# Key tiles turned behind softmax shares, roots written in place, a fifth weight tile and a store on another queue, in a decoder layer on one core

## The chip, the cores and the metric

The kernel runs on 1 core of one Trainium2 chip. The metric is the device time of one execution in microseconds (us). The core has five engines that run side by side, each through its own instruction stream, in order: TensorE (PE, with its weight loads PEld), VectorE (DVE), ScalarE (ACT), GpSimd (POOL) and SyncE (SP), which here only issues transfers. They wait for each other through semaphores.

## The reference

One layer of a hybrid decoder is computed for a prompt of 512 rows and for 8 samples of 4 rows each (32 rows), with the same weights, model width 1024. Cut to what matters:

```python
h = rms_norm(x, g_mix_pre); z = h @ w_in          # mLSTM heads and differential attention read z
mix = concat([mlstm(z), diff_attention(z)])
x = x + rms_norm(mix @ w_out, g_mix_post)
h = rms_norm(x, g_mem_pre)                        # cross-attention, 4 heads x 256, 256 memory tokens
s = einsum('bqhd,bkhd->bhqk', (h @ w_mq), mk) * 256 ** -0.5
x = x + rms_norm((softmax(s) applied to mv) @ w_mo, g_mem_post)
u = rms_norm(x, g_ffn_pre) @ w_up                 # width 2 x 2752, causal depthwise conv of width 3
f = (silu(g) * a) @ w_down
y = x + rms_norm(f, g_ffn_post)
```

where `rms_norm(x, g)` is `x * rsqrt(mean(x * x) + 1e-6) * g`. For the prompt, `mk` and `mv` come from a memory of 256 rows (`rms_norm(mem) @ w_mk`, `@ w_mv`). For each of the 8 samples they are cached: `cache_mem_k` and `cache_mem_v`, 256 tokens x 1024 numbers for each sample. Caches and states are returned too.

## The kernel before, in words

**Order of the work.** The program is written with a tile framework that is told to plan the order by a simulated timeline (L2059, `schedule_with_timeline_sim=True`). What is written earlier has priority, but each engine's final instruction order is the planner's, and it may take an instruction ahead of others if it thinks that its inputs are ready first. Buffers are taken from pools in the same plan. `tc.issue_after(ins)` around a block puts the block's instructions on the engine of `ins` behind `ins` in that engine's order; it adds no wait for another engine. Once planned, the order on each engine is fixed.

**Products.** Each big product is done as three: operands are split into a high part (a cast by ScalarE, L146) and a low part (the difference, by VectorE or GpSimd, L147; the function is `split`), and TensorE multiplies high by high, high by low, low by high (L411 to L413 for w_out and the like, L472 and L485 for the FFN's first product and others).

**Weight tiles.** `Weights` keeps a plan of tiles. A weight piece of 512 KB lands in one of 6 stages (`wst`), is split, and the result (`wslot`) lies in a ring of 4 tiles (pool `wp`, `NSLOT`). A tile's split waits until TensorE has finished with the tile that lay there. A tile marked extra takes a buffer of the large pool `sp` (11 buffers, function `S`) and isn't counted by the ring. Before the change only `slotB` knows that mark; `slotA`, which loads w_out and w_mv in pieces of 256 rows x 512 columns, doesn't. For w_out there are eight tiles: four for columns 0 to 511 and four for 512 to 1023 (L1364 to L1365), all planned after the differential attention (L1257 to L1287: scores `sda`, maximum `nm`, exponentials `pda`, shares at L1265, transposition `tpa`, product `oda`).

**Roots.** `rstd` computes the reciprocal root on GpSimd: L302 forms mean plus epsilon, L304 raises it to the power -0.5 in a small tile `rs`. Two places then copy that column by VectorE into a tile that lives longer: L540 (`mrs`, for the memory's rows, at the start) and L1178 (`rsd`, for the rows ahead of the FFN). There, `norm_turn` transposes a block of rows on TensorE, VectorE scales it into `ht` (L334) and ScalarE casts it into `fT` (L146), which the FFN's first product reads (L472). The roots are not applied there: the rows of `rsd` are spread by small matmuls (L1737) into `rsb`, and VectorE applies them to the product at L1766.

**Cross-attention.** The prompt's part runs in steps: `ch_soft(i)` (scores `sca` L1455, maximum `cnm` L1459, exponentials `cp` L1462, reciprocal L1463, shares L1465), `ch_turn(i - 2)` (transposition `cpt` L1474, split into `pT`) and `ch_out(i - 3)`. The samples' part runs between them: `mk_load(b)` brings the cached keys of sample b (two halves of 128 tokens) into stages or ring tiles (`wst` for b under 3, `kvt` after), `mk_turn(b)` transposes them in place on VectorE in blocks of 32 x 32 (L1508), and `mk_scores` multiplies them with the samples' queries (`ssc`, L1528), for two samples at a time. `mk_sum` and `mem_softmax` follow, and their result is needed before w_mo's tiles find free stages.

**The end.** The last block of 128 rows is finished in pieces of columns: 512 to 767 by ScalarE (L1952) and GpSimd (L1953), 0 to 511 and 768 to 1023 by VectorE (L1955). Each piece's store is issued by SyncE (L1956), in this order of the plan: 0, 768, 512.

Of the kernel before, what the change touches and what calls it, by code (L numbers as in the profile page):

```python
# [15 lines left out]
P = 128  # L16
DM = 1024
# [60 lines left out]
def kernel(ctx: ExitStack, tc: tile.TileContext, I, O):  # L78
# [41 lines left out]
    def small(w, name, p=P):  # L120
        return sm.tile([p, w], F32, name=name, tag=name)
# [5 lines left out]
    def v2(t, b):  # L127
        return t.rearrange("p (a b) -> p a b", b=b)
# [80 lines left out]
    def stage():  # L209
        return stg.tile([P, 1024], F32, name="wst", tag="st")  # L210

    def slot_tile():
        return wp.tile([P, 2, 1024], F32R, name="wslot", tag="W")
# [8 lines left out]
        for e, c in ((nc.vector, slice(0, m)), (nc.gpsimd, slice(m, 2 * m))):  # L222
            e.tensor_tensor(out=sv[:, 1, c], in0=st[:, c], in1=f32(sv[:, 0, c]), op=SUB)

    def slotA(w, k0, n0, nrow=256, share=False):
        def emit():
            st, s = v2(stage(), 512), slot_tile()
            sv = s.rearrange("p l (k n) -> p l k n", k=2)
            r0 = k0 * P
            if nrow == 256:  # L230
                W.last = dma(out=st, in_=w[r0:r0 + 256, n0:n0 + 512].rearrange("(k p) n -> p k n", p=P))
                split_w(sv, st, share)
            else:
                dma(out=st[:, 0, :], in_=w[r0:r0 + P, n0:n0 + 512])
                for p0 in (0, 64):
                    dma(out=st[p0:p0 + 64, 1, :], in_=w[r0 + P:r0 + P + 64, n0:n0 + 512])
                split(sv[:, 0], sv[:, 1], st)
            return sv, st
        W.add(emit)

    def slotsA(w, n0, share=False):
        for k in range(0, 8, 2):
            slotA(w, k, n0, share=share)

    def slotB(w, ranges, share=False, extra=False):
        if extra:
# [48 lines left out]
            o = xt.s[:, 4 * q + j0:4 * q + j1, :]  # L295
            VCP(out=o if len(src.shape) < 4 else o.rearrange("p (h e) n -> p h e n", e=src.shape[2]), in_=src)

    def rstd(ss, n, w, dim, name="rs"):

        r = small(w, name)  # L300
        if dim is not None:
            nc.gpsimd.tensor_scalar(out=r[:n], in0=ss, scalar1=1.0 / dim, scalar2=EPS, op0=MUL, op1=ADD)  # L302
            ss = r[:n]
        GTT(out=r[:n], in0=ss, in1=mhalf[:n, :w], op=ALU.pow)  # L304
        return r[:n]

    def sumsq(x, n, junk, name="ssq"):
        ss = small(1, name)
        ACT(out=junk, in_=x, func=AF.Square, accum_out=ss[:n])
        return ss[:n]  # L310
# [226 lines left out]
                with burst(t):  # L537
                    t = mm(fill, lhsT=warm[:, 0:P], rhs=warm, start=True, stop=True).ins
    for b in range(2):
        VCP(out=mrs[:, b:b + 1], in_=rstd(sumsq(xms[b], P, N("hN")), P, 1, DM))  # L540
    W.nslots = NSLOT
    W.pump()
    def mem_k():
# [575 lines left out]
    def proj_add(xt, gname, src, gname2, dst, order=None, scale=None):  # L1119

        g = gbc(gname)
        y0, s0, xb, pend, ready, target, late = {}, {}, {}, [], [], [], []

        def ssq(b, y, nm):
            n = rows(b)[1]
            ss = sm.tile([P, 1], F32, name=nm, tag=nm, bufs=6)
            j = Z("sqj")
            ACT(out=j[:n], in_=y, func=AF.Square, scale=DM ** -0.5, accum_out=ss[:n])
            return ss[:n]

        def ev0(b, ps):
            n = rows(b)[1]
            z = y0[b] = T2([P, 512], "y0")[:n]
            if b == 4:
                sample_sum(ps, z)
                ps = z
            s0[b] = ssq(b, ps, "ssy0")
            VTT(out=z, in0=ps, in1=g[:n, :512], op=MUL)

        def before(b):  # L1140
            for c in [4, 0, 1, 2, 3] if scale else [b]:
                if c not in xb:
                    xb[c] = N("xb")[:rows(c)[1]]
                    with tc.issue_after(loads) if scale else nullcontext():
                        dma(out=xb[c], in_=src(c))

        def ev1(b, ps):
            c0, n = rows(b)
            z = T2([P, 512], "y1")[:n]
            if b == 4:  # L1150
                sample_sum(ps, z)
                ps = z
            ss = ssq(b, ps, "ssy1")
            VTT(out=z, in0=ps, in1=g[:n, 512:], op=MUL)
            STT(out=ss, in0=s0[b], scalar=EPS, in1=ss, op0=ADD, op1=ADD)
            rs = rstd(ss, n, 1, None)
            late.append((b, z, rs))
            if not scale:
                add(*late.pop(0))

        def add(b, z, rs):
            c0, n = rows(b)
            x = xb[b]
            for i, z in enumerate((y0[b], z)):
                c = slice(512 * i, 512 * i + 512)
                STT(out=x[:, c], in0=z, scalar=rs, in1=x[:, c], op0=MUL, op1=ADD)  # L1166
            dma(out=dst[c0:c0 + n, :], in_=x)
            ready.append((x, n, c0))
            while len(ready) > LR:
                rows_of(*ready.pop(0))  # L1170

        def rows_of(x, n, c0):
            if scale is None:
                pend.append((norm_rows(x, n, ACTROWS), n, gname2, target[0], c0, POOLQ))
                return
            pend.append((x, n, gname2, target[0], c0, POOLQ))
            rs = sm.tile([P, 1], F32, name="rsd", tag="rsd", bufs=5)
            VCP(out=rs[:n], in_=rstd(sumsq(x, n, Z("sqx").bitcast(BF16)[:n]), n, 1, DM))  # L1178
            scale[1].append((rs[:n], c0, n))

        def mid():
            if len(pend) > (0 if scale else LP):
                norm_turn(*pend.pop(0))
            if late:

                with tc.issue_after(scaled[0].ins) if late[0][0] == 2 else nullcontext():
                    add(*late.pop(0))

        def second(xt2):
            target.append(xt2)  # L1190
            run(gemmA(xt, 8, [4, 0, 1, 2, 3], ev1, block_major=True, before=before, mid=mid, midk=1 if scale else MIDK))
            while late:
                add(*late.pop(0))
            while ready:
                rows_of(*ready.pop(0))
            while len(pend) > 2:
                norm_turn(*pend.pop(0))
            return pend
        return gemmA(xt, 8, order or allb, ev0, block_major=order is not None, halves=True), second
# [162 lines left out]
    put(mixT, 1, 0, 4, SEQ, NS, tmp, nc.gpsimd)  # L1362
    F.run()
    for n0 in (0, 512):  # L1364
        slotsA(w_out, n0)  # L1365
    for n0 in (0, 512):
        slotsA(w_mv, n0)
    for m in range(8):
# [73 lines left out]
    run(gemmB(hqT, [ev_q(m) for m in range(4)], half_first=True))  # L1442
    oT = XT("oT")

    pTs, cps, scored = {}, {}, [None]

    def ch_soft(i):
        h, bp = i // 2, i % 2
        sv = v2(mmp("sca"), 256)
        for j in range(2):  # L1450
            t0 = (2 * bp + j) * P
            for c in range(2):
                q, l = qh[h][:, c, t0:t0 + P], ql[h // 2][:, 2 * (h % 2) + c, t0:t0 + P]
                for m, (x, k) in enumerate(((q, 0), (q, 1), (l, 0))):
                    scored[0] = mm(sv[:, j, :], lhsT=x, rhs=mkT[k][:, 2 * h + c, :], start=(c + m == 0),  # L1455
                                   stop=(c == 1 and m == 2))
        nm = small(2, "cnm")
        su = small(2, "csu")
        VRED(out=nm, in_=sv, axis=AX.X, op=MAX, negate=True)  # L1459
        p = cps[i] = v2(Z("cp"), 256)  # L1460
        for j in range(2):
            ACT(out=p[:, j, :], in_=sv[:, j, :], func=AF.Exp, bias=nm[:, j:j + 1], accum_out=su[:, j:j + 1])  # L1462
        nc.vector.reciprocal(out=su, in_=su)  # L1463
        for j in range(2):
            VTS(out=p[:, j, :], in0=p[:, j, :], scalar1=su[:, j:j + 1], scalar2=None, op0=MUL)  # L1465

    def ch_turn(i):
        h, bp = i // 2, i % 2
# [163 lines left out]
    for b in range(0, NB, 2):  # L1632
        t = mk_scores((b, b + 1))
        mv_load(b)
        mv_load(b + 1)
        if b < 6:
            if b:
                mk_turn(b + 2)
            mk_turn(b + 3)
            if b:  # L1640
                next(prompt)
        if b == 4:
            for _ in range(2):
                az.append(N("caz").rearrange("p (h n) -> p h n", h=H))
                nc.gpsimd.memset(az[-1], 0.0)
# [207 lines left out]
    for gi, js in enumerate(groups):  # L1853
# [87 lines left out]
        def end(b):  # L1941
# [3 lines left out]
            if b == TORD[-1]:  # L1945
                VTT(out=yss[b, 0], in0=yss[b, 0], in1=yss[b, 512], op=ADD)
                STT(out=yss[b, 768], in0=yss[b, 0], scalar=EPS, in1=yss[b, 768], op0=ADD, op1=ADD)
                rs = rstd(yss[b, 768], n, 1, None)
                for o, w in ((512, 256), (0, 512), (768, 256)):
                    c, z = slice(o, o + w), zs[b, o]  # L1950
                    if o == 512:
                        nc.scalar.mul(out=z, in_=z, mul=rs)  # L1952
                        GTT(out=xb[:, c], in0=xb[:, c], in1=z, op=ADD)  # L1953
                    else:
                        STT(out=xb[:, c], in0=z, scalar=rs, in1=xb[:, c], op0=MUL, op1=ADD)  # L1955
                    dma(out=out[:, c], in_=xb[:, c])  # L1956
                return
            STT(out=yss[b, 512], in0=yss[b, 0], scalar=EPS, in1=yss[b, 512], op0=ADD, op1=ADD)
            rs = rstd(yss[b, 512], n, 1, None)
# [103 lines left out]
```

## Time and profile before

| what | value |
|---|---|
| runs | 935.85, 933.4 and 934.09 us, median 934.09 |
| profiled execution, its own time | 933.45 us |
| its span, first to last instruction | 931.7 us |
| around the span | 1.75 us |
| granted TensorE clock, mean | 0.996 |
| TensorE busy | 913.5 us, 98% |
| VectorE busy | 606.5 us, 65% |
| ScalarE busy | 377.7 us, 41% |
| GpSimd busy | 223.0 us, 24% |

All times of the profile are counted from the span's start. A row of a timeline gives start, length, engine, line, operation, what it writes from what it reads, how many instructions are drawn together, and in brackets how long the engine stood idle before it and what ended that. A row of waits gives the engine and line that waited, what it waited for, the total in us, how many times, and the longest. A busy time is the union of an engine's instructions, so that two instructions that overlap are not counted twice; VectorE's instructions overlap by some hundredths of a microsecond.

### The profile page before, as it was taken

The page shows a single profiled execution, that of the slowest core. Times are in us where ns is not written, and L with a number is a line of the kernel's source. Part 1 is how long each engine was busy: PE and PEld are TensorE (multiplying, and loading weights), DVE is VectorE, ACT ScalarE, POOL GpSimd, SP SyncE. Part 2 cuts the span into 40 slices and gives each one's busy share as a digit, 9 for nine tenths or more (in the row PEclk, how much of TensorE's full clock was granted, in tenths as well). Part 3 has the DMA queues.
Part 4 walks back from the last instruction along what each step waited for, and adds up shares of the span by engine and source line. Part 5 has one row for each costly group of instructions (what it writes and reads, how often), then busy time and mean ns, then how long its engine had stood idle before and what let it go on. Part 6 is the DMA issues. An engine that isn't in the chain of part 4 may idle for free. (4 is left out here: it accounts for less than half of the span.)

```text
span 931.7 us, 17473 instructions
## 1 busy us (share of the span) xinstructions
PE 913.5 (98%) x6780; PEld 797.6 (86%) x6780; DVE 606.5 (65%) x1128; ACT 377.7 (41%) x728; POOL 223.0 (24%) x475
## 2 busy tenths in 40 slices
PE   9999999999999999999999999999999999999995
PEld 6899787879866778998877899899888998999974
DVE  5845144565888338768645878547748775776767
ACT  5745233344587437724534533322212221222232
POOL 6611000034442126581000642001001110110114
PEclk9999999999999999999999999999999999999998
DMA  9960023335780439966777631152044304412023
GB/s 284 313 192 4 1 91 139 91 102 164 237 294 19 136 107 293 300 214 236 293 244 194 200 108 53 38 168 69 27 137 137 91 4 131 122 47 91 25 94 118
DMA packets 120834, 130.59 MB, mean 140 GB/s; under 512 B 8599, under 2 KB 86264, under 8 KB 120752
## 3 DMA queue, kind: packets, MB, share of 16 engines
q1 hardware_dynamic: 114568, 125.96, 42.9%
q10 hardware_dynamic: 6184, 3.53, 1.2%
q8 instruction: 53, 0.87, 0.4%
q14 instruction: 29, 0.24, 0.1%
HBM read 112.54 MB, written 16.93 MB: 139 GB/s over the span
## 5 line engine op out<-in xcount | busy, mean ns | idle before, releaser
L485 PE MATMUL mm<-fT,wslot 128*128 128x256 f32 x1872 | 235.9, 288 | 0.0
L485 PEld LDWEIGHTS mm<-fT,wslot 128*128 128x128 f32 x1872 | 234.4, 188 | 1.8 <-issue 0.8
L146 ACT CAST wslot<-wst 128x1024 fp32r<-128x1024 f32 x125 | 130.4, 1049 | 255.0 <-issue 72.5
L147 DVE TENSOR_TENSOR wslot<-wst,wslot 128x1024 fp32r<-128x1024 f32 x125 | 154.2, 1239 | 76.1 <-ACT wslot L146 75.7
L1869 PE MATMUL mm<-wslot,act 128*128 128x512 f32 (+1 forms) x180 | 69.3, 387 | 0.0
L1872 PE MATMUL mm<-wslot,act 128*128 128x512 f32 (+1 forms) x172 | 67.1, 391 | 0.0
L1873 PE MATMUL mm<-wslot,act 128*128 128x512 f32 (+1 forms) x172 | 66.8, 392 | 0.0
L1771 POOL COPY cvo<-u 128x2 f32<-128x2 f32 x43 | 10.4, 242 | 217.4 <-DVE u L1769 217.4
L411 PE MATMUL mm<-wslot,hT 128*128 128x512 f32 x128 | 51.3, 402 | 0.0
L413 PE MATMUL mm<-wslot,hT 128*128 128x512 f32 x128 | 51.0, 399 | 0.0
L485 PE MATMUL mm<-hT,wslot 128*128 128x256 f32 (+1 forms) x384 | 50.9, 289 | 0.0
L412 PE MATMUL mm<-wslot,hT 128*128 128x512 f32 x128 | 50.8, 397 | 0.0
L1766 DVE TENSOR_TENSOR u<-mm,rsb 128x256 f32<-128x256 f32 x43 | 18.1, 424 | 48.4 <-PE mm L485 48.4
L485 PEld LDWEIGHTS mm<-hT,wslot 128*128 128x128 f32 x384 | 49.2, 188 | 0.5 <-issue 0.2
L1869 PEld LDWEIGHTS mm<-wslot,act 128*128 128x128 f32 x180 | 34.3, 191 | 8.0 <-issue 0.4
L1873 PEld LDWEIGHTS mm<-wslot,act 128*128 128x128 f32 x172 | 32.3, 188 | 6.9 <-issue 0.4
L1872 PEld LDWEIGHTS mm<-wslot,act 128*128 128x128 f32 x172 | 32.3, 188 | 6.9
L1783 ACT ACTIVATE c<-c 128x560 f32<-128x560 f32 x21 | 14.1, 672 | 57.2 <-DVE c L1777 57.1
L1777 DVE SCALAR_TENSOR_TENSOR c<-u,cvT,c 128x560 f32<-128x560 f32 x43 | 34.4, 799 | 0.9
L1776 DVE SCALAR_TENSOR_TENSOR c<-u,cvT,c 128x560 f32<-128x560 f32 x43 | 34.1, 794 | 0.2
L1884 DVE TENSOR_TENSOR yp<-mm,yp 128x512 f32<-128x512 f32 (+1 forms) x41 | 27.1, 673 | 4.5 <-PE mm L1873 4.3
L413 PEld LDWEIGHTS mm<-wslot,hT 128*128 128x128 f32 x128 | 24.1, 188 | 5.0
(497 smaller groups left out, 1857.5 us busy)
## 6 DMA issues: line engine op xcount, KB each, us to landing
wst<-in_w_up_dram SPq DMA_DIRECT2D x42, 512.0 KB
wst<-in_w_in_dram SPq DMA_DIRECT2D x28, 512.0 KB
wst<-in_w_down_dram SPq DMA_DIRECT2D x20, 512.0 KB
kvt<-in_cache_mem_k_dram SPq DMA_DIRECT2D x10, 512.0 KB
kvt<-in_cache_mem_v_dram SPq DMA_DIRECT2D x10, 512.0 KB
wst<-in_w_mk_dram SPq DMA_DIRECT2D x8, 512.0 KB
xb<-in_x_prompt_dram SPq DMA_DIRECT2D x8, 512.0 KB
wst<-in_cache_dk_dram SPq DMA_DIRECT2D x16, 256.0 KB
```

The source lines that it names most:

```text
L146: nc.scalar.copy(out=hi, in_=src)
L147: (eng or nc.vector).tensor_tensor(out=lo, in0=src, in1=f32(hi), op=SUB)
L411: mm(ps[b], lhsT=xt.hi(k, c0, c0 + n), rhs=s[:, 0, kk, :], start=(k == 0), stop=False)
L412: mm(ps[b], lhsT=xt.hi(k, c0, c0 + n), rhs=s[:, 1, kk, :], start=False, stop=False)
L413: return mm(ps[b], lhsT=xt.lo(k, c0, c0 + n), rhs=s[:, 0, kk, :], start=False, stop=(k == nk - 1))
L485: mm(ps[i], lhsT=s[:, l, k, :], rhs=x(k, c0, c1), start=(k == 0 and j == 0), stop=(k == 7 and j == 2))
L1776: STT(out=c, in0=u[:, 1:EXT - 1], scalar=w[1], in1=c, op0=MUL, op1=ADD)
L1777: STT(out=c, in0=u[:, 0:EXT - 2], scalar=w[0], in1=c, op0=MUL, op1=ADD)
L1869: mm(ps, lhsT=t[:, 0, c0:c0 + P], rhs=s[:, 0, i % 2, cs], start=st, stop=False)
L1872: mm(ps, lhsT=t[:, 0, c0:c0 + P], rhs=s[:, 1, i % 2, cs], start=False, stop=False)
L1873: return mm(ps, lhsT=t[:, 1, c0:c0 + P], rhs=s[:, 0, i % 2, cs], start=False, stop=en)
L1884: VTT(out=y, in0=ps, in1=y, op=ADD)
```

## The change

It has four parts.

1. `rstd` takes an output. At L540 and L1178 GpSimd writes the reciprocal roots straight into `mrs` and `rsd`; VectorE's two and five copies of one column are gone.
2. `slotA` and `slotsA` know the mark extra. The first tile of w_out's second half (rows 0 to 255 of columns 512 to 1023) takes a buffer of the large pool and no ring tile.
3. The transpositions of the cached keys of samples 3 to 7 are put behind a prompt step's shares in VectorE's order: sample 3 behind those of step 1, samples 4 and 5 behind step 2, samples 6 and 7 behind step 3. `ch_soft` keeps its last share instruction in `shares` for that.
4. The store of columns 768 to 1023 of the last block is issued by ScalarE and not by SyncE.

```diff
+    def slotA(w, k0, n0, nrow=256, share=False, extra=False):
+        if extra:
+            W.extra.add(len(W.plan))
+
         def emit():
-            st, s = v2(stage(), 512), slot_tile()
+            st, s = v2(stage(), 512), S([P, 2, 1024], F32R, "wslot") if extra else slot_tile()
...
-    def slotsA(w, n0, share=False):
+    def slotsA(w, n0, share=False, extra=False):
         for k in range(0, 8, 2):
-            slotA(w, k, n0, share=share)
+            slotA(w, k, n0, share=share, extra=extra and k == 0)
...
-    def rstd(ss, n, w, dim, name="rs"):
-
-        r = small(w, name)
+    def rstd(ss, n, w, dim, name="rs", out=None):
+
+        r = small(w, name) if dim is not None or out is None else None
         if dim is not None:
             nc.gpsimd.tensor_scalar(out=r[:n], in0=ss, scalar1=1.0 / dim, scalar2=EPS, op0=MUL, op1=ADD)
             ss = r[:n]
-        GTT(out=r[:n], in0=ss, in1=mhalf[:n, :w], op=ALU.pow)
-        return r[:n]
+        out = r[:n] if out is None else out
+        GTT(out=out, in0=ss, in1=mhalf[:n, :w], op=ALU.pow)
+        return out
...
-        VCP(out=mrs[:, b:b + 1], in_=rstd(sumsq(xms[b], P, N("hN")), P, 1, DM))
+        rstd(sumsq(xms[b], P, N("hN")), P, 1, DM, out=mrs[:, b:b + 1])
...
-            VCP(out=rs[:n], in_=rstd(sumsq(x, n, Z("sqx").bitcast(BF16)[:n]), n, 1, DM))
+            rstd(sumsq(x, n, Z("sqx").bitcast(BF16)[:n]), n, 1, DM, out=rs[:n])
...
     for n0 in (0, 512):
-        slotsA(w_out, n0)
+        slotsA(w_out, n0, extra=n0 > 0)
...
-            VTS(out=p[:, j, :], in0=p[:, j, :], scalar1=su[:, j:j + 1], scalar2=None, op0=MUL)
+            shares[i] = VTS(out=p[:, j, :], in0=p[:, j, :], scalar1=su[:, j:j + 1], scalar2=None, op0=MUL)
...
         if b < 6:
-            if b:
-                mk_turn(b + 2)
-            mk_turn(b + 3)
+            with tc.issue_after(shares[b // 2 + 1].ins):
+                if b:
+                    mk_turn(b + 2)
+                mk_turn(b + 3)
...
-                    dma(out=out[:, c], in_=xb[:, c])
+                    (nc.scalar.dma_start if o == 768 else dma)(out=out[:, c], in_=xb[:, c])
```

More of the change, by code (lines that the diff above doesn't have):

```diff
@@ L223, in split_w @@
             e.tensor_tensor(out=sv[:, 1, c], in0=st[:, c], in1=f32(sv[:, 0, c]), op=SUB)
-    def slotA(w, k0, n0, nrow=256, share=False):
+    def slotA(w, k0, n0, nrow=256, share=False, extra=False):
+        if extra:
+            W.extra.add(len(W.plan))
         def emit():
-            st, s = v2(stage(), 512), slot_tile()
+            st, s = v2(stage(), 512), S([P, 2, 1024], F32R, "wslot") if extra else slot_tile()
             sv = s.rearrange("p l (k n) -> p l k n", k=2)
@@ L1443 @@
     oT = XT("oT")
-    pTs, cps, scored = {}, {}, [None]
+    pTs, cps, scored, shares = {}, {}, [None], {}
     def ch_soft(i):
```

## The prediction

> **What bounds the kernel now.** I read the page's busy times first, then the same busy times stretch by stretch, then TensorE's waits.
>
> ```profile
> span 931.7 us, 17473 instructions
> PE 913.5 (98%) x6780; PEld 797.6 (86%) x6780; DVE 606.5 (65%) x1128; ACT 377.7 (41%) x728; POOL 223.0 (24%) x475
> ```
>
> TensorE is busy for 913.5 of 931.7 us. The change takes no matmul away, so all that can be won lies in the 18.2 us in which TensorE stands still. The busy times by stretch (columns: stretch, length, then busy time and instruction count of PE, PEld, DVE, ACT and POOL, granted clock, DMA share, GB/s) say where those are:
>
> ```profile
> 250.00:300.00 50.00, 47.76 (x456) 33.36 (x454) 43.76 (x111) 39.95 (x127) 17.27 (x22) 1.00 0.56 192
> 300.00:350.00 50.00, 49.71 (x280) 38.83 (x280) 20.05 (x33) 20.63 (x44) 11.18 (x13) 1.00 0.36 118
> 400.00:450.00 50.00, 49.28 (x671) 46.87 (x670) 38.77 (x65) 19.50 (x68) 20.66 (x74) 1.00 0.69 247
> 900.00:931.70 31.70, 20.23 (x104) 16.30 (x102) 24.37 (x41) 11.32 (x30) 14.09 (x13) 0.89 0.28 103
> ```
>
> The tail holds 11.5 us, the attention stretch 2.2, the stretch of the cached keys 0.7, the output projection 0.3. TensorE's waits (us in total, times, longest) name the ones that this change can touch:
>
> ```profile
> PE tpa L1273 <- DVE pda L1265: 1.4, 2, 1.1
> PE cpt L1474 <- DVE cp L1465: 0.7, 1, 0.7
> PE mm L412 <- DVE wslot L223: 0.4, 1, 0.4
> PE mm L412 <- DVE wslot L147: 0.3, 1, 0.3
> PE mm L472 <- ACT fT L146: 0.3, 1, 0.3
> ```
>
> Four of these five (all but the first) stand in front of work that an edit makes earlier: 0.7 + 0.4 + 0.3 + 0.3 = 1.7 us. That is the ceiling inside the body; the tail comes on top.
>
> **Part 1, roots written in place.** Seven VectorE copies of one column go away (two at L540, five at L1178). At the start only this one matters, and this one near the FFN's start:
>
> ```profile
> 12.54 0.14 DVE L540 COPY mrs<-rs 128x1 f32<-128x1 f32 x1
> 12.60 1.31 DVE L223 TENSOR_TENSOR wslot<-wst,wslot 128x512 fp32r<-128x512 f32 x1
> 537.32 0.75 DVE L1766 TENSOR_TENSOR u<-mm,rsb 128x256 f32<-128x256 f32 x2
> 539.01 0.16 DVE L1178 COPY rsd<-rs 128x1 f32<-128x1 f32 x1 [0.95 <-POOL rs L304]
> 539.08 1.28 DVE L334 TENSOR_TENSOR ht<-tp,gT 128x512 f32<-128x512 f32 x2
> 540.47 0.79 PE L472 MATMUL mm<-fT,wslot 128*128 128x288 f32 x4 [0.29 <-ACT fT L146]
> ```
>
> At 12.54 the copy starts 0.06 us before the next instruction: VectorE overlaps its instructions, so the start-to-start distance is the price. The 0.4 us wait for wslot L223 shrinks by **0.06**. At 539.01 it is not the copy's 0.16 us that costs. VectorE is in order: the copy waits 0.95 us for GpSimd's root, and ht behind it, which needs no root (it scales with gT), waits too. Without the copy, ht starts 0.9 to 1.0 us earlier, ScalarE's cast behind it likewise, and the 0.29 us wait of L472 goes: **0.29**. What is late next is the row sum on TensorE that reads rsd; it goes by the same GpSimd root as now, and the copy's time is taken off its way. The other five copies lie where TensorE doesn't wait: 0.
>
> **Part 2, one more weight tile.** The w_out tile that takes a buffer of the large pool needs no tile of the four-tile ring; the tiles behind it get their ring tile one release earlier. The wait it aims at:
>
> ```profile
> 337.36 1.05 ACT L146 CAST wslot<-wst 128x1024 fp32r<-128x1024 f32 x1 [4.15 <-PE mm L413]
> 338.44 1.22 DVE L147 TENSOR_TENSOR wslot<-wst,wslot 128x1024 fp32r<-128x1024 f32 x1 [5.88 <-ACT wslot L146]
> 339.72 0.50 PE L412 MATMUL mm<-wslot,mixT 128*128 128x512 f32 x1 [0.29 <-DVE wslot L147]
> ```
>
> The cast waited 4.15 us for TensorE to free a ring tile, then cast and difference took 1.05 + 1.22 us, and TensorE came 0.29 us too soon. One release earlier is far more than 0.29: **0.29** gained. Against it, the extra tile's cast and difference no longer wait for the ring and may move forward into the attention stretch, where VectorE is busy 43.76 of 50 us and TensorE already waits for it (L1265, 1.4 us). Its price there is between 0 (it falls into one of VectorE's 6.2 idle us) and 1.22 (it stands whole ahead of a softmax step for which TensorE waits). Nearest are the first four of these tiles, done in that stretch (mean 1.22 us, 0.1 us idle before all of them), with no wait of a matmul put down to them:
>
> ```profile
> L147 DVE TENSOR_TENSOR wslot<-wst,wslot 128x1024 fp32r<-128x1024 f32 x4 | 4.8, 1221 | 0.1
> 266.53 1.06 DVE L1265 SCALAR_TENSOR_TENSOR pda<-pda,rc 128x256 f32<-128x256 f32 x1
> 266.28 1.04 POOL L1103 TENSOR_TENSOR dasq<-dao,dars 128x512 f32<-128x512 f32 x1
> ```
>
> So I take 0.2 near the low end; net gain **0.1**. The last two rows show what would make it dearer: beside a GpSimd operation of 1.04 us a VectorE operation took 1.06. [...]
>
> **Part 3, the cached keys behind the shares.** VectorE now turns key tiles of batches 3 and 4 early, in time it has to spare, and two of batch 6 just ahead of a prompt step's shares:
>
> ```profile
> 415.86 1.25 DVE L1508 STREAM_TRANSPOSE kvt<-kvt 128x1024 f32<-128x1024 f32 x1 [2.05 <-DMA kvt<-in_cache_mem_k_dram]
> 421.27 2.51 DVE L1508 STREAM_TRANSPOSE kvt<-kvt 128x1024 f32<-128x1024 f32 x2 [2.02 <-DMA kvt<-in_cache_mem_k_dram]
> 432.07 1.22 DVE L1508 STREAM_TRANSPOSE kvt<-kvt 128x1024 f32<-128x1024 f32 x1
> 433.21 0.63 DVE L1465 TENSOR_SCALAR cp<-cp,csu 128x256 f32<-128x256 f32 x2
> 438.94 0.60 DVE L1465 TENSOR_SCALAR cp<-cp,csu 128x256 f32<-128x256 f32 x2
> 433.71 0.74 PE L1474 MATMUL cpt<-cpk,cp 128*128 128x128 f32 x4 [0.67 <-DVE cp L1465]
> 442.40 1.97 PE L1528 MATMUL ssc<-kvt,qx 128*32 128x128 f32 x64
> 447.78 1.96 PE L1528 MATMUL ssc<-kvt,qx 128*32 128x128 f32 x64
> ```
>
> The transposition at 432.07 (1.22 us) holds the shares, and TensorE waits 0.67 us for them. Held behind the shares, it stands in nobody's way there: up to **0.7** won. But the edit ties all ten: batch 3 to step 1's shares (end 433.84), batches 4 and 5 to step 2's (439.54), 6 and 7 to step 3's. The 2 × 1.25 + 2.51 = 5.0 us of batches 3 and 4, done for nothing at 415 to 424, come into this:
>
> ```profile
> 428.00:432.00 4.00, 4.00 (x38) 3.87 (x40) 4.00 (x6) 1.07 (x5) 0.10 (x1) 1.00 0.63 201
> 432.00:436.00 4.00, 3.33 (x93) 2.95 (x95) 4.00 (x10) 3.68 (x16) 1.91 (x9) 1.00 0.58 234
> 436.00:440.00 4.00, 3.95 (x165) 3.24 (x157) 3.87 (x9) 2.71 (x12) 0.86 (x1) 1.00 0.64 213
> 440.00:444.00 4.00, 4.00 (x72) 3.44 (x76) 2.50 (x6) 2.31 (x7) 0.00 (x0) 1.00 1.00 398
> 444.00:448.00 4.00, 4.00 (x52) 3.66 (x44) 1.75 (x5) 2.31 (x9) 0.00 (x0) 1.00 1.03 416
> ```
>
> VectorE's 4.00 + 4.00 + 3.87 + 2.50 + 1.75 = 16.1 us become 21.1 in 20 us, before the last key scores at 447.78. Three things ease it: the shares come earlier by at least the 1.22 us of the transposition that is taken from ahead of them, TensorE can take a later step's prompt scores first, and splits that nobody needs yet can slip past 448. Queued behind a held transposition are the splits of the prompt's scores and the next maximum. So the part's result lies between -0.7 and +2.0 (batches 4 and 5 begun only at 439.54 end at 439.54 + 4 × 1.22 = 444.4, where TensorE wants them at 442.40); I take a gain of **0.3**, nearer the wait that certainly goes, less some of the 1.1 us that VectorE lacks.
>
> **Part 4, the last store.** SyncE issues all three pieces of the last block, in program order:
>
> ```profile
> 926.66 1.61 DVE L1955 SCALAR_TENSOR_TENSOR xf<-zy,rs,xf 128x512 f32<-128x512 f32 x2 [0.73 <-POOL rs L304]
> 927.24 0.75 POOL L1953 TENSOR_TENSOR xf<-xf,zy 128x256 f32<-128x256 f32 x1 [0.62 <-ACT zy L1952]
> L1956 SPq DMA_DIRECT2D out_dram<-xf x3: 332/332/403, 927.4 to 928.7; - x3
> SPq L2059 <- DMA out_dram<-xf: 1.4, 2, 0.9
> ```
>
> VectorE's pieces are ready at 927.4 and 926.66 + 1.61 = 928.27, GpSimd's at 927.99, and an issue takes 0.33 to 0.40 us; yet the last issue starts at 928.7, because one store queues behind the other. With ScalarE's queue taking one (ScalarE has no work left then), the last issue starts at 928.3: **0.4** earlier, and the end, which waits only for the stores, follows. Bounds: 0 (the transfers share bandwidth anyway) to 0.5.
>
> **Sum.** 0.06 + 0.29 + 0.1 + 0.3 + 0.4 = 1.15 us. The profiled execution took 933.45 us; the runs' median is 934.09, 0.64 above. So 932.3 against the profiled one and 932.9 against the median; I forecast 932.6, the middle. About 0.3%, 2.8 us, is what a measurement of this kernel tells from no change, and this is less.
>
> **Rivals.** All start from 933.75, the middle of the two times.
>
> *The transpositions pile up (slower).* The planned order holds batches 4 and 5 to 439.54 or later: 2.0 us at 442.40, and of the 1.1 us that VectorE lacks about half at 447.78, so +2.5 instead of -0.3. With the other parts' 0.85: 933.75 + 2.5 - 0.85 = 935.4. It decides once step 2's shares end after 442.40 - 4.9 = 437.5. For it: the full VectorE row of 428 to 440. Against it: the shares come earlier by what is taken from ahead of them.
>
> *The whole order is planned anew (faster).* The planner places every engine's work by a simulated time; one tile and seven copies less can shift much. The attention stretch's 2.2 us of standstill are the largest lump outside the tail, and the wait of L1273 is VectorE's order alone. If that goes, 932.6 - 2.2 = 930.4; the same mechanism may lose as much.
>
> *The extra tile costs its 1.22 in the attention stretch.* 932.6 + 1.0 = 933.6.
>
> *The change does nothing that lasts.* Each wait won is met again by the next one, or the transfers of the last block end as before: 933.75.
>
> **How the numbers follow.** Forecast 0.55 (own range 931.5 to 933.7), pile-up 0.20, anew and faster 0.12, extra tile dear 0.08, nothing 0.05. Faster by over 0.3% of the median (below 931.3) takes in nearly all of the third and an edge of the first, since four waits by TensorE's own gaps may be worth a little more than the rows say: 0.24. Slower by over 0.3% (above 936.9) needs the pile-up beyond 2.5 or a lost order: 0.12. Within: 0.64. The range from 930.4 to 936.0 leaves out half of the faster rival and the upper part of the pile-up.
>
> **What would show it.** Part 1: no copy at L1178, ht starting near 538.1, no wait of L472. Part 2: no wait of L412 for L147 near 339; wrong if TensorE is less busy than 47.76 in 250 to 300. Part 3: no wait of cpt L1474 for cp L1465; wrong if the key scores L1528 wait for a transposition or VectorE is idle at 415 to 424 and TensorE at 436 to 452. Part 4: one store on ScalarE's queue and the last issue near 928.3 on the old scale. The forecast as a whole is wrong if TensorE's standstill is not 0.8 to 1.6 us shorter.

## The result

The changed kernel takes 939.59 us (median; 938.96 to 941.09), the kernel before 934.14 us: a ratio of 1.006, 95% interval 1.0044 to 1.0076. It is slower by 5.5 us, where 1.5 us faster was forecast, and it lies above the range. Its page of the profile begins:

```profile
span 938.0 us, 17461 instructions
PE 916.1 (98%) x6780; PEld 799.9 (85%) x6780; DVE 606.3 (65%) x1121; ACT 378.1 (40%) x728; POOL 217.9 (23%) x475
```

TensorE has the same 6780 matmuls but is busy 2.6 us longer, and it stands still 21.9 us, not 18.2. The same stretches as before (length, busy time and count of PE, PEld, DVE, ACT and POOL, granted clock, DMA share, GB/s), with the one between them added: first its row in the kernel before, then the changed kernel's rows, and under them a finer cut of the place:

```profile
350.00:400.00 50.00, 50.00 (x319) 45.09 (x318) 36.97 (x47) 35.95 (x55) 30.94 (x41) 1.00 0.92 295
...
300.00:350.00 50.00, 50.00 (x284) 39.42 (x283) 19.97 (x34) 18.74 (x43) 10.35 (x10) 1.00 0.35 116
350.00:400.00 50.00, 46.66 (x266) 40.90 (x265) 35.62 (x47) 34.39 (x50) 22.00 (x26) 0.93 0.89 277
400.00:450.00 50.00, 49.45 (x590) 48.21 (x589) 31.91 (x51) 17.66 (x57) 24.97 (x91) 1.00 0.61 215
...
378.00:380.00 2.00, 0.45 (x4) 0.46 (x5) 2.00 (x3) 2.00 (x3) 0.00 (x0) 1.00 0.85 340
380.00:382.00 2.00, 0.69 (x7) 0.45 (x5) 2.00 (x4) 2.00 (x4) 0.03 (x1) 0.82 0.05 18
382.00:384.00 2.00, 2.00 (x9) 2.00 (x10) 2.00 (x2) 2.00 (x4) 2.00 (x2) 0.50 0.64 190
388.00:390.00 2.00, 2.00 (x19) 2.00 (x18) 1.74 (x3) 1.63 (x4) 1.23 (x2) 0.98 0.89 285
```

The new loss lies at 376 to 390, a stretch of which the prediction says nothing: 3.3 us of standstill, and behind it some 7 us at a granted clock of 0.50. TensorE's waits:

```profile
PE tp L336 <- ACT hN L320: 1.8, 1, 1.8
PE mm L476 <- ACT hqT L146: 1.6, 2, 1.3
PE tpa L1277 <- DVE pda L1269: 1.4, 2, 1.1
PE mm L416 <- DVE wslot L223: 0.6, 1, 0.6
PE ssc L1532 <- issue: 0.6, 1, 0.6
```

Three of the four waits that were to go are gone (cpt for cp, mm for wslot L147, mm for fT); the fourth, for wslot L223, went from 0.4 to 0.6 us. At the top stand two new ones: TensorE waits for the normed rows `hN` and for the input `hqT` of w_mq's products.

To see where the traces part, I compare when each stage's first product starts. A row gives line, what it writes from what it reads, how many, then the shortest, median and longest in ns, then the first and the last start in us. In the first trace of the kernel before, then in that of the changed one:

```profile
L472 PE MATMUL mm<-hqT,wslot x192: 277/291/364, 378.3 to 402.9; 128*128 128x256 f32 x96, 128*128 128x288 f32 x96
L1455 PE MATMUL sca<-mkT,qh x64: 277/282/387, 418.0 to 457.8; 128*128 128x256 f32 x64
L411 PE MATMUL mm<-wslot,oT x64: 389/396/499, 473.1 to 524.8; 128*128 128x512 f32 x64
L1869 PE MATMUL mm<-wslot,act x180: 278/389/499, 589.3 to 919.7; 128*128 128x512 f32 x172, 128*128 128x256 f32 x8
```

```profile
L476 PE MATMUL mm<-hqT,wslot x192: 277/294/582, 381.9 to 410.1; 128*128 128x256 f32 x96, 128*128 128x288 f32 x96
L1459 PE MATMUL sca<-mkT,qh x64: 274/281/385, 425.2 to 464.7; 128*128 128x256 f32 x64
L415 PE MATMUL mm<-wslot,oT x64: 389/395/504, 480.0 to 531.8; 128*128 128x512 f32 x64
L1874 PE MATMUL mm<-wslot,act x180: 278/389/499, 595.8 to 926.2; 128*128 128x512 f32 x172, 128*128 128x256 f32 x8
```

The changed kernel is late by 3.6 us at w_mq, by 7.2 at the prompt's scores, by 6.9 at w_mo and by 6.5 at the down projection. All of the loss arises between 376 and 425; behind that it wins a little back. About half of it, 3.5 us, arises within w_mq's products, which begin at the lower clock: from their first product to the prompt's first scores it takes 39.7 us before and 43.2 here.

**What became late.** ScalarE's first operations behind the output projection's first half (start, length, what, idle before), before and then after; `sqj` is the sum of squares for that half's last block:

```profile
337.36 1.05 ACT L146 CAST wslot<-wst 128x1024 fp32r<-128x1024 f32 x1 [4.15 <-PE mm L413]
339.71 0.59 ACT L1128 ACTIVATE sqj<-mm 128x512 f32<-128x512 f32 x1
```

```profile
340.68 1.05 ACT L146 CAST wslot<-wst 128x1024 fp32r<-128x1024 f32 x1 [6.94 <-PE mm L417]
343.03 0.60 ACT L1132 ACTIVATE sqj<-mm 128x512 f32<-128x512 f32 x1
```

Everything here is 3.3 us late, and it waits for TensorE, which was not standing still. So TensorE did something else first. TensorE's planned order of w_out's products, one entry for each uninterrupted run of one block's products, 24 for a block and half:

```
            first half, last block   second half, three blocks, ahead of its last 12
before      12 ... 12                12 + 12 + 12   (contraction blocks 0 to 3)
after       12 ... 2, 10             18 + 18 + 14   (contraction blocks 0 to 5)
```

The extra tile lies ready early, so contraction blocks 4 and 5 of the second half can be multiplied, and the planner puts 50 products, not 36, ahead of the last 12 of the first half: 14 more at 0.23 us, 3.2 us. (The traces agree: when that block's sum of squares starts, 135 of the 192 products have ended before, 148 in the changed kernel.) On ScalarE, in order, the sum of squares of that block comes 3.3 us later, and behind it queue the copies of the sample rows, their sums and the normed rows. The work of TensorE is the same in sum, but what hangs on that block isn't.

### The profile page after: what moved, and what is told of

Same layout as the page of the kernel before. It is cut to its first block, busy times and chain, and to the rows that moved or that the text cites. A ratio compares the mean times of both kernels' runs of the same rounds, so it can differ in the third digit from the quotient of the medians.

```text
span 938.0 us, 17461 instructions
## 1 busy us (share of the span) xinstructions
PE 916.1 (98%) x6780; PEld 799.9 (85%) x6780; DVE 606.3 (65%) x1121; ACT 378.1 (40%) x728; POOL 217.9 (23%) x475
## 4 chain that ended last, share of the span: by engine, by line
PE 88%; DVE 5%; DMA 3%; ACT 2%; issue 1%; POOL 0%; ACTq 0%; DVEq 0%; SPq 0%; POOLq 0%
PE mm L489 33%; PE mm L415 7%; PE mm L416 7%; PE mm L417 7%; PE mm L476 7%; PE mm L1874 4%; PE mm L1878 3%; PE mm L1877 3%; PE mm L394 2%; PE sda L1261 1%; PE sca L1459 1%; PE cpo L1490 1%; PE sdn L394 1%; PE ssc L1532 1%; PE oda L1289 1%
## 5 line engine op out<-in xcount | busy, mean ns | idle before, releaser
L147 DVE TENSOR_TENSOR wslot<-wst,wslot 128x1024 fp32r<-128x1024 f32 x125 | 154.3, 1239 | 80.3 <-ACT wslot L146 80.0
L1771 DVE TENSOR_TENSOR u<-mm,rsb 128x256 f32<-128x256 f32 x43 | 18.2, 424 | 49.2 <-PE mm L489 48.4
L476 PE MATMUL mm<-hqT,wslot 128*128 128x256 f32 (+1 forms) x192 | 27.5, 309 | 1.6 <-ACT hqT L146 1.6
```

What stands on the lines that cost most here:

```text
L147: (eng or nc.vector).tensor_tensor(out=lo, in0=src, in1=f32(hi), op=SUB)
L476: done[0] = mm(ps, lhsT=s[:, l, k, :], rhs=x(k, c0, c1), start=(k == 0 and l == 0 and x == xt.hi), stop=(k == 7 and x == xt.lo))
```

## The experiments

The ratio is to the kernel before on the same chip, with its 95% interval. There the kernel before had medians of 934.05 to 934.51 us; the ratio is not the quotient of the two medians.

| kernel | median us | ratio |
|---|---|---|
| all four parts (the change) | 939.59 | 1.0060 (1.0044 to 1.0076) |
| part 2 alone | 939.0 | 1.0047 (1.0034 to 1.0061) |
| without part 2 | 933.58 | 0.9985 (0.9976 to 0.9995) |
| part 3 alone | 934.51 | 0.9998 (0.9989 to 1.0007) |
| parts 1 and 4 alone | 934.01 | 0.9990 (0.9981 to 0.9999) |
| all four, products held | 934.81 | 1.0003 (0.9994 to 1.0012) |
| all four, last tile extra | 935.28 | 1.0007 (0.9998 to 1.0015) |
| 1, 4, samples 6 and 7 behind step 1 | 936.44 | 1.0016 (1.0006 to 1.0025) |
| the same with 64 small matmuls at the start | 940.65 | 1.0066 (1.0053 to 1.0080) |
| 1 and 4 with 32, 64, 96 small matmuls | 936.08, 936.46, 935.93 | 1.0022, 1.0025, 1.0015 |

### Which part costs it

Theories: A, the extra tile by TensorE's running ahead; B, the sum of the edits through a new plan; C, part 3. Part 2 alone (the calls; `slotA` and `slotsA` as in the change):

```diff
-        slotsA(w_out, n0)
+        slotsA(w_out, n0, extra=n0 > 0)
```

> The kernel before with part 2 alone. Theory A (the extra tile lets TensorE run second-half products of w_out ahead of the first half's last block; that block's sums, the norm rows and hqT come some 3 us later and TensorE stands still ahead of w_mq, then runs at a lower granted clock): the loss is all here, TensorE's standstill of about 3 us near 376 to 382 and granted clock near 0.5 behind it, time 6 to 8 us above the kernel before, 940 to 942. Theory B (no single part; the order is planned anew by the sum of the edits): the standstill ahead of w_mq isn't there or is another, time within 3 us of before. Theory C (the held transpositions cost the time): no loss, 933 to 934.

Measured 939.0, less than the 940 to 942 of theory A. TensorE's standstills in the stretch:

```profile
378.78 1.09 PE L335 MATMUL tp<-cpk,hN 128*128 128x128 f32 x8 [0.95 <-ACT hN L319]
381.18 9.85 PE L475 MATMUL mm<-hqT,wslot 128*128 128x256 f32 x81 [1.31 <-ACT hqT L146]
394.99 5.30 PE L475 MATMUL mm<-hqT,wslot 128*128 128x288 f32 x38 [1.23 <-ACT hqT L146]
```

The loss is here, the standstill too, but the granted clock is not: it stays at 1.00 in this trace, and a third wait of 1.23 us stands where the changed kernel ran slowly. So the lower clock is not what makes the kernel slower; it can come on top. From w_mq's first product to the prompt's first scores it takes 41.6 us here and 43.2 in the changed kernel, so I estimate the lower clock at 1.6 us in that trace. Of the changed kernel's runs one had a mean clock of 0.996 and 938.96 us, the others 0.993 to 0.994 and 939.44 to 941.09; four runs don't settle its price.

The changed kernel without part 2 (`extra=n0 > 0` taken out again):

> The changed kernel without part 2 (parts 1, 3 and 4 stay). Theory A: no standstill ahead of w_mq and granted clock 1.0 there; the gains of 0.4 at the FFN's start and 0.4 at the last store are left, and what part 3 does, so 932 to 934.5. Theory B: still 3 us or more above before. Theory C: 938 to 940, as with all four parts.

Measured 933.58, ratio 0.9985: 1.4 us faster than before by the ratio (0.5 by the medians on that chip), and faster than the changed kernel by 6. Theory A holds, B and C fall as the cause of the loss. Part 2 alone loses 4.4 us and the other parts win 1.4, which makes 3.0 and not the 5.5 measured; the lower clock may be a part of the difference, and the rest is open. This is the fastest kernel measured, though parts 1 and 4 alone, below, can't be told from it.

### Part 3 alone, and parts 1 and 4 alone

Part 3 alone (`shares` as in the change):

```diff
-            if b:
-                mk_turn(b + 2)
-            mk_turn(b + 3)
+            with tc.issue_after(shares[b // 2 + 1].ins):
+                if b:
+                    mk_turn(b + 2)
+                mk_turn(b + 3)
```

> The kernel before with part 3 alone. As forecast: TensorE's wait of 0.7 us for the shares is gone, the last key scores may be up to 1 us late; 0.3 us gained, 933.8, with a range from 0.7 gained to 2.5 lost. Theory A: nothing else changes ahead of 400 us. Theory C: 4 us or more above before.

> The kernel before with parts 1 and 4 alone; they lie at 0 to 25, 510 to 545 and behind 925 us and can be read apart in one trace. As forecast: 0.06 at the start, 0.3 to 0.4 at the FFN's start, 0.4 at the end gained, 0.7 to 0.9 in all, 933.3. Theory B: a changed order at the start costs some tenths, or more elsewhere; within 1 us of before or above it.

Part 3 makes no difference that can be measured (934.51, 0.9998). Parts 1 and 4 together win 0.1% by the ratio (0.9990, barely clear of 1; the medians, 934.01 and 934.05, don't show it). Both traces start 0.6 to 1.0 us late against the first trace of before, and both have a standstill in the key scores that ends with no wait, which the first trace doesn't have. That made the first trace itself doubtful, hence the second trace of the unchanged kernel below.

### Run-ahead or shifted ring

Theory A has two forms: A1, the products that run ahead; A2, the ring that is shifted by one tile and brings w_mv's loads and casts ahead of others. Two kernels keep the shift and take the run-ahead away. The first holds the second half's later products behind the first half's last one, in order only (the passing on of the list `hold` is left out):

```diff
+                    late = hold and mid and b < 4 and k >= 4
+                    with tc.issue_after(hold[0]) if late else nullcontext():
+                        t = one(b, k, slots[k // 2])
+                    if hold is not None and not mid and b == blocks[-1] and k == nk - 1:
+                        hold.append(t.ins)
```

> The changed kernel with all four parts, and with the products of w_out's second half for contraction blocks 4 to 7 put behind the first half's last product in TensorE's order, as it was before. The extra tile, its ring shift, its loads and its casts stay. Theory A1 (TensorE runs some 12 matmuls of 0.23 us ahead of the first half's last block, and everything that hangs on that block comes 3 us late): the sums of squares on ScalarE come back to near 340, no standstill ahead of w_mq, time 2 us or more below the changed kernel down to that of the changed kernel without the extra tile, 932.5 to 934. Theory A2 (the shifted ring puts loads and casts of w_mv ahead of the prompt rows' and memory keys' loads, which then come late): the standstill stays, 938 to 940.

The second makes the last tile of w_out the extra one:

```diff
-            slotA(w, k, n0, share=share, extra=extra and k == 0)
+            slotA(w, k, n0, share=share, extra=extra and k == 6)
```

> The changed kernel with all four parts, but the last tile of w_out's second half (contraction blocks 6 and 7) takes the large pool's buffer, not the first. The ring is shifted by one tile as in the change, but TensorE can't run past contraction block 3 ahead of the first half's last block: the planned order has 12 products each of three blocks ahead of it, as in the kernel before, not 18, 18 and 14. Theory A1 (run-ahead): no standstill of 3 us ahead of w_mq, ScalarE's sum of squares for the first half's last block near 340, time 933 to 935, as with the held order. Theory A2 (shifted ring): the standstill is there, 938 to 940.

Measured 934.81 and 935.28, against 939.59; A1 gave 932.5 to 934 and 933 to 935, so both are 0.3 to 0.8 us above it. In both, the planned order has 12 + 12 + 12 ahead again, and ScalarE's sum of squares comes at 341.03 and 341.38 in traces that start 1.0 and 1.4 us late: where it was, to 0.3 us. The waits for `hN` are gone, of those for `hqT` 0.33 us is left in the first of them:

```profile
341.03 0.59 ACT L1136 ACTIVATE sqj<-mm 128x512 f32<-128x512 f32 x1
391.85 8.32 PE L480 MATMUL mm<-hqT,wslot 128*128 128x288 f32 x59 [0.33 <-ACT hqT L146]
```

A1 is shown twice; A2 falls as the cause of the 5 us. A rest remains: with the order held, the extra tile is still 0.2% behind the kernel without it (1.0003 against 0.9985). In the trace 0.3 us of it lie in the attention stretch, where the extra tile's cast falls, and the rest in w_mq's products; I did not take that further.

### The key scores: a second trace of before, and one transposition only

> The kernel before, unchanged, for a second trace. If the lag of 0.1 to 1.0 us at the start of the other traces, and the standstills in the run of key scores that end with no wait, vary from one execution to the next, this trace differs from the first by as much there and agrees within 0.1 us elsewhere. If they belong to the changed programs, it has neither.

The unchanged kernel's second trace: 935.34 us, span 933.6, not 931.7. The first trace was an early one. It starts w_in's products, the first of the layer, and the rest 0.97 us sooner, and its wait of 0.67 us for the shares does not occur in the second, although the transposition stands ahead of the shares there as well:

```profile
432.22 1.22 DVE L1508 STREAM_TRANSPOSE kvt<-kvt 128x1024 f32<-128x1024 f32 x1
433.37 0.64 DVE L1465 TENSOR_SCALAR cp<-cp,csu 128x256 f32<-128x256 f32 x2
433.87 0.74 PE L1474 MATMUL cpt<-cpk,cp 128*128 128x128 f32 x4
437.86 0.47 PE L1528 MATMUL ssc<-wst,qx 128*32 128x64 f32 x18 [0.54 <-issue]
444.86 1.28 PE L1528 MATMUL ssc<-kvt,qx 128*32 128x128 f32 x36 [0.73 <-issue]
```

TensorE arrives a microsecond later and finds the shares ready; instead it stands still twice inside a run of key scores, for 0.54 and 0.73 us, with nothing that it waits for. Only samples 6 and 7 held, with parts 1 and 4:

```diff
-            if b:
-                mk_turn(b + 2)
-            mk_turn(b + 3)
+            with tc.issue_after(shares[1].ins) if b == 4 else nullcontext():
+                if b:
+                    mk_turn(b + 2)
+                mk_turn(b + 3)
```

> Parts 1 and 4, and of part 3 only this: the keys of samples 6 and 7 are turned behind the shares of step 1; samples 3 to 5 are turned freely as before. Theory A (part 3's loss is the pile-up of the early transpositions of samples 3 and 4, its gain the one transposition ahead of step 1's shares): the wait of 0.7 for the shares is gone and nothing is late; 0.5 to 0.9 us below parts 1 and 4 alone, 932.5 to 933.3. Rival (TensorE's standstills in the run of key scores that end with no wait have another cause than the transpositions): the wait goes, but 0.5 to 1.5 us of such standstill stay, and the time is that of parts 1 and 4 alone.

Neither came: 936.44, slower than parts 1 and 4 alone by 2.4 us. The transpositions are in time, but TensorE's standstills in the key scores grow to 3.4 us:

```profile
440.06 1.30 PE L1529 MATMUL ssc<-kvt,qx 128*32 128x128 f32 x40
443.89 1.28 PE L1529 MATMUL ssc<-kvt,qx 128*32 128x128 f32 x24 [2.53 <-issue]
```

Forty matmuls of one run, then 2.53 us of nothing, then the other 24. Behind it the granted clock was 0.50 for 3.4 us, which costs more time (stretches of 2 us, columns as above; the two that hold the slow part take in its ends):

```profile
442.00:444.00 2.00, 0.11 (x5) 0.11 (x8) 0.00 (x0) 0.00 (x0) 0.00 (x0) 1.00 0.99 387
444.00:446.00 2.00, 2.00 (x26) 1.52 (x24) 0.00 (x0) 0.74 (x2) 0.00 (x0) 0.55 1.02 416
446.00:448.00 2.00, 2.00 (x7) 1.52 (x7) 0.69 (x1) 0.59 (x1) 0.00 (x0) 0.60 1.07 426
```

Two theories: I, instructions that come late; W, a wait that the profile doesn't name. The packets of I are in the page, the lateness isn't: in the changed kernel's, as in that of before, the queue q8 of instructions moved 53 packets, 0.87 MB, so 16.4 KB each. That they are TensorE's is an estimate from the count: 6780 matmuls and 6780 weight loads are 256 for each packet, 259 with the semaphore waits. Small matmuls at the very start shift all later instructions:

```diff
+    for _ in range(64):
+        mm(wps[:32, :32], lhsT=warm[:, 0:32], rhs=warm[:, 0:32], start=True, stop=True)
```

> The kernel with samples 6 and 7 behind step 1 and parts 1 and 4, with 64 more matmuls of 32x32 at the very start, where TensorE waits for the first loads; nothing of the planned order changes behind the first 30 us. They move the rest of TensorE's instruction stream by 128 instructions. Theory I (the standstills without a wait in the key scores are late instructions: they come in packets of 16 KB, 256 instructions, and a dense run eats a packet faster than the next arrives): the standstills move to other matmuls of the run, or vanish, and their sum changes from 3.4 us; the time moves by 1 us or more, either way. Theory W (they are waits for a transposition that the profile doesn't name): they stay at the same matmuls, 0.9 and 2.5 us, and the time stays at 936.4.

The time rose to 940.65, for a reason of its own: the planner arranged the first 30 us anew and lost there. But the key scores have no standstill left. The first products of the layer, the key scores and w_mo's products, without and with the 64:

```profile
L473 PE MATMUL mm<-hT,wslot x192: 277/292/386, 36.2 to 64.4; 128*128 128x256 f32 x96, 128*128 128x288 f32 x96
L1529 PE MATMUL ssc<-kvt,qx x160: 269/273/421, 437.4 to 452.3; 128*32 128x128 f32 x160
  issue: 3.4, 2
L412 PE MATMUL mm<-wslot,oT x64: 389/394/504, 476.8 to 528.5; 128*128 128x512 f32 x64
```

```profile
L475 PE MATMUL mm<-hT,wslot x192: 276/292/388, 44.7 to 72.6; 128*128 128x256 f32 x96, 128*128 128x288 f32 x96
L1531 PE MATMUL ssc<-kvt,qx x160: 270/273/298, 444.8 to 455.8; 128*32 128x128 f32 x160
L414 PE MATMUL mm<-wslot,oT x64: 387/394/504, 480.4 to 532.4; 128*128 128x512 f32 x64
```

8.5 us late at the start, 3.6 us late at w_mo: 4.9 us won in between, with the same order of the same work from 65 us on. From the prompt's first scores to w_mo's first product it takes 54.0 us, not 58.7: 3.4 of these 4.7 us are the standstills, and the lower clock behind them, which this trace doesn't have there, can account for the rest. Three more kernels put small matmuls behind the first half of w_mq's products, in parts 1 and 4 alone, where no engine's order of anything else changes (32 here, 64 and 96 in the others):

```diff
     pS = at("pS")[:, :256]
+    t = done[0].ins
+    for _ in range(32):
+        with burst(t):
+            t = mm(pS[:32, :32], lhsT=warm[:, 0:32], rhs=warm[:, 0:32], start=True, stop=True).ins
```

> Parts 1 and 4 alone, with 32 more matmuls of 32x32 put right behind the first half of w_mq's products; every other instruction stands in the same order on every engine. They cost about 32 x 7 ns = 0.2 us of TensorE. Theory I (late instructions): TensorE's standstills without a wait in the key scores, 0.9 and 0.2 us without them, move by 64 instructions and change in length. Theory W (unnamed waits): they stay where they are.

> The same with 64 matmuls, 0.45 us. Theory I: half a packet of 256 instructions; the standstills change most, to none or to 1.5 us and more, time between 932.5 and 935.5. Theory W: as without, plus 0.45 us, 934.5.

> The same with 96 matmuls, 0.7 us. Theory I: another length of the standstills than with 32 and 64. Theory W: as without, plus 0.7 us, 934.7.

The standstills in the key scores go from 1.1 us to none with 32, 0.2 us with 64 and none with 96. From the prompt's first scores to w_mo's first product it takes 55.4 us without them (419.0 to 474.4), and 54.0, 54.8 and 53.9 with them. All the same, no time was won: the small matmuls started 25 ns apart, not the 7 that I expected (the 32 took 0.96 us to the end of the last), so TensorE's next product came 0.9 to 2.5 us after the first of them, for at most 1.5 us won; and with 32 and 64 another 1.3 us went at the FFN's start, in these traces, by a wait of 1.0 us for `fT` whose cause I did not look for.

That the standstills go does not refute W yet: the small matmuls also make TensorE arrive later, and what it waited for may then be ready. The places decide. The breaks without small matmuls, and with 64 of them:

```profile
437.99 0.47 PE L1529 MATMUL ssc<-wst,qx 128*32 128x64 f32 x18 [0.85 <-issue]
444.43 1.29 PE L1529 MATMUL ssc<-kvt,qx 128*32 128x128 f32 x36 [0.20 <-issue]
```

```profile
440.70 0.25 PE L1529 MATMUL ssc<-wst,qx 128*32 128x64 f32 x2 [0.24 <-issue]
```

Count TensorE's instructions (matmuls, weight loads and semaphore waits) from the start of the trace. The two breaks stand at numbers 6337 and 6593, 256 apart. In all traces together there are 19 standstills of over 0.1 us between 430 and 465 us that end with no wait, in 10 of the 14, 16 of them among the key scores and 3 among the prompt's scores beside them; all lie at 6337 or 6338, 6593 or 6594, 6849 or 6850. The one with 64 small matmuls lies at 6594 as well, although another score stands there than without them. So the place in the instruction stream decides and not the work, every 256 instructions, and W falls.

Theory I is borne out as far as this. That the packets themselves come late is argued: no row shows it. The 256 between the places agree with the 256 to 259 for each packet of q8; the standstills add up to as much as 3.4 us in a stretch of 15 us, if the packets are the cause. Why four of the traces have no such standstill there, with the same places in their streams, stays open.

## Why the prediction was wrong, and where it was right

**Part 2 was the step that failed**, at the sentence "One release earlier is far more than 0.29: 0.29 gained". It priced the tile's cast and difference, and asked whether they collide with the attention; it didn't ask what TensorE does with a tile that is ready earlier. It ran 14 products ahead, and a block on which the next stage's rows hang came 3.2 us later; TensorE then stood still for 3.1 us ahead of w_mq, 1.79 for `hN` and 1.31 for `hqT`. The terms that were priced came out nearly as forecast: the 0.29 us was won (TensorE is busy for all 50 us of 300 to 350), and the tile's price in the attention was 0.3 to 0.4 us, not 0.2 (from w_in's first product to w_out's first it takes 263.3 and 263.4 us in the two traces with this tile, 263.0 before). Its difference took 1.22 us at 272.1, as the other four did, although GpSimd operations of 1.55 and 1.80 us ran beside it (270.52 and 272.02), so GpSimd did not make it dearer. In place of the 0.1 us gained the part costs 4.4 us alone (ratio 1.0047).

**The rival that the order is planned anew** named the mechanism in general and said that it "may lose as much", but gave that side no time and no chance of its own, so the range ended at 936.0. The chance of slower by over 0.3% was put at 0.12.

**Part 1** was right at the FFN's start: from w_mo's first product to the down projection's first it takes 116.2 us before and 115.8 in the changed kernel (0.4, by the rows above; forecast 0.29), and the wait for `fT` is gone. The mechanism is there too: the last pair of `ht` starts 66.0 us after w_mo's first product before and 64.7 in the changed kernel, 1.3 us earlier (0.9 to 1.0 forecast). The 0.06 us at the start can't be seen: the start differs by up to 1 us between two executions of the same kernel.

**Part 3** aimed at a wait, "the wait that certainly goes", that the second trace of before doesn't have. The gain of 0.3 isn't there, and neither is the pile-up: the last key scores came in time in every trace, and part 3 alone measures 0.9998 (934.51, with an uncertainty of about 0.8 us). The length of this stretch goes mostly with the standstills with no wait: 55.1 us (none, but the wait for the shares) and 56.0 (1.3 us of them) in the two traces of before, and from 53.9 (none) to 58.7 (3.4) in the others.

**Part 4** was right in mechanism and near in size. The last store is issued by ScalarE (start and length of the issues, and of the last pieces on VectorE):

```profile
933.32 1.61 DVE L1960 SCALAR_TENSOR_TENSOR xf<-zy,rs,xf 128x512 f32<-128x512 f32 x2 [0.73 <-POOL rs L308]
934.10 0.91 SPq L1961 DMA_DIRECT2D out_dram<-xf  x2
934.97 0.34 ACTq L1961 DMA_DIRECT2D out_dram<-xf  x1
```

The last issue starts 0.04 us after the last piece's end (934.93), not 0.4 us as before. From that end to the end of the span it takes 3.0 to 3.1 us in the ten traces with part 4, and 3.4 in the four without: about 0.3 won, 0.4 forecast. The three stores do share the 16 DMA engines, which were 79% busy from 928.26 to 930.15 before and 96% from 934.93 to 936.42 in the changed kernel; 0.3 was won all the same.

Without part 2 the sum of the other parts was forecast at 0.06 + 0.29 + 0.3 + 0.4 = 1.05 us; measured are 1.4 (0.5 to 2.2). That the forecast for these was near is partly luck, since part 3's share wasn't there.

## What to carry to other kernels

- A buffer that makes work ready sooner also lets an engine do it sooner, ahead of work on which more depends. Before giving a producer more room, ask what the consumer will run first with it, and what is then late; where the order is planned, hold it.
- A wait of half a microsecond in a single trace may be slack: take a second trace of the unchanged kernel before aiming at it.
- When one part of a change loses and the others gain, undo the parts one by one: here one lost 4.4 us, two together won about 0.1%, and one made no difference that could be measured.

## What the runs showed of the hardware

- Dense runs of small matmuls (four key scores, one in each column group, start 7 ns apart, and the next four 56 ns after them with 64 columns, 109 ns with 128) stood still for 0.2 to 2.5 us with no wait, in 10 of 14 traces, and only at places 256 instructions apart in TensorE's stream. With 64 small matmuls put ahead, another score stood at such a place. One kernel with the same order took 54.0 us in this stretch and not 58.7.
- Two standstills of 1.79 and 1.31 us within 4.2 us were followed by 6.8 us at a granted clock of 0.50; with 0.95 and 1.31 us at the same place, in the kernel with part 2 alone, the clock stayed at 1.00. One of 2.53 us among the key scores, with one of 0.92 us four us ahead of it, was followed by 3.4 us at 0.50. What length of standstill lowers the clock these three cases don't settle.
- Matmuls of 32 columns started 25 ns apart, one behind the other (32 of them took 0.96 us to the end of the last). The key scores, in four column groups, come closer: with 64 columns four of them start within 56 ns, 14 ns each.
